# A state-space mixer's scan on one core: output tables moved behind the input tables, chunk inputs copied two groups at a time, a scan step of four full-width operations

## The chip, the cores and the metric

The kernel runs on one core of one Trainium2 chip. The metric is the device time of one execution in microseconds (us); the kernel before takes 2886.24 us (median of 3 runs, 2885.1 to 2886.93). Engines are named as in the profile: PE (TensorE matmul; PEld its weight loads), DVE (VectorE), ACT (ScalarE), POOL (GpSimd), SP (the queue that issues most DMAs). L353 means line 353 of the kernel.

## The reference, cut to what matters

The model is a two-layer encoder on 1040 tokens of width 1024. The change touches only the token mixer of layer 0, a bidirectional S5 state-space mixer. For each of 64 groups (16 channels, 64 complex states) and for each of two directions:

```
abar = exp(lambda * dt)                 # one complex number per group and state
bbar = (abar - 1) / lambda * b          # 64 x 16, complex
s[l] = abar * s[l-1] + bbar @ u[l]      # the scan over tokens l; the second direction runs backwards
y[l] = Re(c @ s[l])                     # summed over both directions
y    = y + d_skip * u, then GELU, a GLU and a projection
```

Everything behind it (GLU, projection, layer norms, SwiGLU, grouped-query attention, a second SwiGLU) is untouched.

## The kernel before, in words

The 1040 tokens are cut into NK = 130 chunks of T = 8. Within a chunk, the effect of inputs on outputs is a small matrix per group; across chunks a state per group is carried. All of that is `s5_phase` (L114 to L550), which runs alone at the start of the program; the rest of the kernel follows it. The order of instructions on each engine is the order in which the program issues them (written out by hand), and each engine works through its own list in order, waiting on semaphores for data and for buffers.

`s5_phase` has these stages.

1. **Parameters.** DVE computes `abar` and the coefficients into `AC`. PE transposes inputs (`x_main`, `x_tail`), the raw `b` and `c` parameters (`param_T`) and `AC`; ACT copies the results out of PSUM. DVE builds the powers of `abar` (`PW`, by `cmul`) and from them the input tables `G3` (`tables`, L299). POOL adds `Br` and `Bi` into `Hs` (L252). The two raw parameters share one buffer, so `raw_c` is loaded into it after `raw_b` has been transposed.
2. **Input side, 16 batches of four groups** (loop at L394). In batch `gb`: `x_main` transposes inputs (batches 2 to 9 only; `xg_copy` stages them on ACT in batches 1 to 8); `g_batch(gb + 1)` multiplies out the next batch's input matrices (five DVE operations of 128x512, L335 to L339, eight PE transposes, two ACT copies into `W`); `x_batch(gb)` multiplies `W` with the inputs `U` on PE (L353, L355: forward and backward halves, one PSUM bank a group), and ACT copies each group's result into `XS[:, k, c, g]`, the chunk inputs (L357, 128x258 each, four a batch). `XS` has the group as its last index, so each of these copies writes single 4-byte values 256 bytes or more apart.
3. **Output tables** (`out_side`, L367, on POOL): the sum `Cs`, a complex product into `PC` (`cmul`, six operations of 128x512) and four operations of `tables` into `E3`, with two ACT copies. It is issued in batches 1 and 6 of stage 2. From `E3` and `c`, `e_batch` (five POOL operations of 128x512, L386 to L390) makes the output matrices of four groups. Four of the 16 `e_batch` calls (EARLY) are issued in batch 10 of stage 2, the other twelve inside the scan.
4. **Scan** (L489): 128 dependent steps over the chunks, `i` = 2 to 129, on DVE. The state has 128 partitions (64 states of each direction) and, per partition, 2 x 64 values (real and imaginary part of 64 groups). A step is cut into two halves of 32 groups, six operations:

```
for h, gs in enumerate(halves):
    V.tensor_tensor(out=TA[:, h], in0=SB[:, :, :, gs], in1=bc(st[:, :, gs], 1, 2), op=ALU.mult)
for h, gs in enumerate(halves):
    V.tensor_tensor(out=bi[:, :, gs], in0=TA[:, h, 0], in1=bi[:, :, gs], op=ALU.add)
for h, gs in enumerate(halves):
    V.tensor_tensor(out=nx[:, :, gs], in0=bi[:, :, gs], in1=TA[:, h, 1, ::-1], op=ALU.add)
```

   `SB` (the real part twice, and plus and minus the imaginary part of `abar` to the eighth) and `bi` (the chunk inputs, copied four chunks at a time by ACT into `IN`, L484, two buffers) lie in PSUM; `TA`, `st` and `nx` lie in SBUF. So every operation of a step reads one operand from PSUM and one from SBUF.
   Beside the scan, POOL makes the output matrices (`e_batch`, paced by E_PACE steps), and for each batch `inside` computes the within-chunk part: POOL `dI` (L424), PE (L433), ACT copies (L439 to L441), POOL adds (L442, L443), eight DMAs `M0` on SP (L449), PE (L455), an ACT copy into `U` (L460). Its parts come 2, 6, 8, 18 and 21 steps after its start, which is at step 3 + 6.2 `gb`. In the second half of the scan `swap` turns the backward direction's states round, through a PSUM bank, on ACT.
5. **Output** (L528): PE multiplies the states with the output matrices (L534, 256 matmuls), DVE adds them to `U`, and the result goes to DRAM and back for GELU.

PSUM has eight banks: five for general use (`s5_ps`), three for `SB` and the two `IN` buffers.

Of the kernel before, what the change touches and what calls it, by code (L numbers as in the profile page):

```python
# [9 lines left out]
FP32 = mybir.dt.float32  # L10
# [3 lines left out]
ALU = mybir.AluOpType  # L14
# [4 lines left out]
KT = 8  # L19
G = 64  # L20
LATE_FT = 4
EARLY = 4
Y_AT = 18
X_AT, E_AT = 2, 10
E_PACE, L_PACE = 7.9, 6.2
CH = 16
T = 8
NK = L // T
# [2 lines left out]
def bc(ap, dim, n):  # L31

    a = ap.unsqueeze(dim)
    shape = list(a.shape)
    shape[dim] = n
    return a.to_broadcast(shape)
# [77 lines left out]
def s5_phase(nc, tc, P, a, ident, acc, xres, ydram, late):  # L114

    V, A, PE, PO = nc.vector, nc.scalar, nc.tensor, nc.gpsimd
    ps = P("s5_ps", bufs=5, space=PSUM)

    psc = P("s5_psc", space=PSUM)

    def bank(name="b"):
        return ps.tile([128, 512], FP32, tag="b", name=name)
# [70 lines left out]
    def x_tail():  # L193
        b = bank()
        transpose(b[:, :128], XT.rearrange("p t c -> p (t c)"))
        A.copy(out=U[:, :, 128:130], in_=b[:, :128].rearrange("p (k g) -> p g k", k=2))

    def param_T(x, raw):

        PT = tab.tile([128, 2, G, CH], FP32, name=x + "T")  # L200
        for h in range(4):
            b = bank()
            for c4 in range(4):
                c = 4 * h + c4
                transpose(b[:, c4 * 128:c4 * 128 + 128], raw[:, c::CH] if x == "b" else raw[:, c * 128:c * 128 + 128])
            A.copy(out=PT[:, :, :, 4 * h:4 * h + 4], in_=b.rearrange("p (c i g) -> p i g c", c=4, g=G))
        return PT[:, 0], PT[:, 1]
# [38 lines left out]
                lst[i]()  # L246
    for p in range(4):
        x_main(p, XG0[:, 4 * p:4 * p + 4])
    Br, Bi = param_T("b", raw_b)
    x_tail()  # L250
    Hs = tab2.tile([128, G, CH], FP32, name="Hs")
    PO.tensor_tensor(out=Hs, in0=Br, in1=Bi, op=ALU.add)  # L252
    AC = pc.tile([64, 4, 128], FP32, name="AC")
    cm, nr, sh, sn, t1, t2, rden = (t[n] for n in ("cm", "nr", "sh", "sn", "t1", "t2", "rden"))
    V.scalar_tensor_tensor(out=cm, in0=sh, scalar=-2.0, in1=sh, op0=ALU.mult, op1=ALU.mult)
# [25 lines left out]
    PO.memset(PW[:, 1, 0], 0.0)  # L281
    V.tensor_copy(out=PW[:, :, 1], in_=b[:, :128].rearrange("p (k g) -> p k g", k=2))
    A.copy(out=acT, in_=b[:, :256].rearrange("p (k g) -> p k g", k=4))
    P.close("s5_pc")
    XG1 = xg_copy(4, 4)
    for p in range(4):
# [28 lines left out]
    A.copy(out=dsk, in_=b[:CH, :G])  # L315
    Cs = tab.tile([128, G, CH], FP32, name="Cs")

    SB = psc.tile([128, 512], FP32, name="SB")[:, :256].rearrange("p (j c g) -> p j c g", j=2, g=G)
    A.copy(out=SB[:, 0], in_=bc(PW[:, 0, 8], 1, 2))
    A.copy(out=SB[:, 1, 0], in_=PW[:, 1, 8])  # L320
    A.mul(SB[:, 1, 1], PW[:, 1, 8], -1.0)


    xs_p = P("s5_xs", side="right")
    XS = xs_p.tile([128, NK, 2, G], FP32, name="XS")
# [20 lines left out]
        return W  # L346

    def x_batch(gb, W):
        for j in range(NB):
            b = bank()  # L350
            g = NB * gb + j
            for c2 in range(2):
                PE.matmul(b[0:64, c2 * NK:c2 * NK + NK - 1], W[:, j, c2, 0:64], U[:, g, 0:NK - 1],  # L353
                          start=True, stop=True)
                PE.matmul(b[64:128, c2 * NK:c2 * NK + NK - 1], W[:, j, c2, 64:128], U[:, g, NK - 1:0:-1],  # L355
                          start=True, stop=True)
            A.copy(  # L357
                out=XS[:, 1:NK, :, g].rearrange("p k c -> p c k"),
                in_=b[:, :2 * NK].rearrange("p (c k) -> p c k", c=2)[:, :, :NK - 1],
            )  # L360


    PC = pw_p.tile([128, 2, T, G], FP32, name="PC")
# [1 line left out]
    s2 = w2.rearrange("p (n g) -> p n g", g=G)  # L365

    def out_side():  # L367
        PO.tensor_tensor(out=Cs, in0=Cr, in1=Ci, op=ALU.add)
        cmul(nc, PC[:, 0], PC[:, 1], PW[:, 0, 0:8], PW[:, 1, 0:8], bc(acT[:, 2], 1, T), bc(acT[:, 3], 1, T), s1, s2, eng=PO)
        yield from tables(PO, E3, PC, slice(0, 8), slice(7, None, -1), -1)  # L370

    NG = G // NB
    ek = tab.tile([128, NB, T, CH], FP32, name="ek")
# [16 lines left out]
        PO.tensor_tensor(out=ei, in0=ei, in1=ek, op=ALU.subtract)  # L390

    W = g_batch(0)
    side = out_side()
    for gb in range(NG):  # L394
        p = 8 + gb - X_AT
        if 8 <= p < NG:
            x_main(p, nxg)
        if gb in (1, 6):
            next(side, None)
        if gb == E_AT:  # L400
            P.close("s5_xg", "s5_in", "s5_xin")
            Eh[0] = P("s5_e0", side="right").tile([128, 2, G // 2, T, CH], FP32, name="E0")
            for b in range(EARLY):
                e_batch(b)
        Wn = g_batch(gb + 1) if gb + 1 < NG else None
        if 7 <= p < NG - 1:
            nxg = xg_copy(p + 1, 1)
        x_batch(gb, W)
        W = Wn
    for q in range(4):  # L410
        dst = xres[q * 256:q * 256 + 256].rearrange("(g c) t k -> t c g k", c=CH)
        for t in range(T):
            nc.sync.dma_start(out=dst[t], in_=U[16 * t:16 * t + 16, 16 * q:16 * q + 16, :])
    P.close("s5_pw", "s5_g", "s5_tab2")


    Eh[1] = P("s5_e1", side="right").tile([128, 2, G // 2, T, CH], FP32, name="E1")
    rp = P("s5_r")
    TA = rp.tile([128, 2, 2, 2, G // 2], FP32, name="TA")
    def inside(gb):  # L420

        gs = slice(NB * gb, NB * gb + NB)
# [39 lines left out]
    def swap(lo, hi):  # L462

        n = hi - lo
        t = bank().rearrange("p (k c g) -> p k c g", c=2, g=G)[64:, :n]
        m0, m1 = NK - hi, NK - lo
        A.copy(out=t, in_=XS[64:, lo:hi])
        yield
        for cs, cp in [(slice(0, 2), A.copy)] if lo else [(slice(0, 1), A.copy), (slice(1, 2), V.tensor_copy)]:
            cp(out=XS[64:, lo:hi, cs], in_=XS[64:, m1 - 1:m0 - 1 if m0 else None:-1, cs])  # L470
            cp(out=XS[64:, m0:m1, cs], in_=t[:, ::-1, cs])
# [2 lines left out]
    cuts = [65, 61, 57, 53, 49, 45, 41, 37, 33, 29, 25, 21, 17, 13, 10, 7, 4, 0]  # L474
    sw = [(lo, hi) for hi, lo in zip(cuts, cuts[1:])]
    begun = []
    halves = [slice(0, G // 2), slice(G // 2, G)]
    IN = {}

    def inputs(i):  # L480
# [7 lines left out]
    inputs(2)  # L488
    for i in range(2, NK):  # L489
        for gb in range(NG):  # L490
            if i == 2 + int(E_PACE * (gb - EARLY)):
                e_batch(gb)
            l0 = 3 + int(L_PACE * gb)
            if i == l0:
                work[gb] = [inside(gb), l0]
        for gb in list(work):
            if i >= work[gb][1]:
                at = next(work[gb][0], None)
                if at is None:
                    del work[gb]  # L500
                else:
                    work[gb][1] = 3 + int(L_PACE * gb) + at
        if i % 4 == 2 and i + 4 < NK:
            inputs(i + 4)
        st, nx, bi = XS[:, i - 1], XS[:, i], IN.pop(i)
        for h, gs in enumerate(halves):
            V.tensor_tensor(out=TA[:, h], in0=SB[:, :, :, gs], in1=bc(st[:, :, gs], 1, 2), op=ALU.mult)  # L507
        for h, gs in enumerate(halves):
            V.tensor_tensor(out=bi[:, :, gs], in0=TA[:, h, 0], in1=bi[:, :, gs], op=ALU.add)  # L509
        for h, gs in enumerate(halves):  # L510
            V.tensor_tensor(out=nx[:, :, gs], in0=bi[:, :, gs], in1=TA[:, h, 1, ::-1], op=ALU.add)  # L511
        if sw and len(begun) < 2 and i > NK // 2:
            begun.append((sw[0][0], swap(*sw.pop(0))))
            next(begun[-1][1])
        while begun and NK - 1 - begun[0][0] <= i - 1:
            next(begun.pop(0)[1], None)
    for gb in list(work):
        for _ in work.pop(gb)[0]:
# [9 lines left out]
    for ft in range(KT):  # L528
# [11 lines left out]
        if ft % 2:  # L540
# [4 lines left out]
            if ft < LATE_FT:  # L545
                for f in (ft - 1, ft):
                    ys[f] = load_y(nc.scalar, y_p, ydram, f)
                for f in (ft - 1, ft):
                    gelu(nc, acc, ys[f], f)
    P.close("s5_e1", "s5_e0", "s5_xs", "s5_psc", "s5_ps", "s5_y")  # L550


def load_y(eng, pool, src, ft, tag="y"):
# [1036 lines left out]
```

## Time and profile before

| | |
|---|---|
| median of 3 runs | 2886.24 us |
| the profiled execution, its own time | 2882.8 us |
| its span, first to last instruction | 2881.0 us |
| busy share of the span | PE 92%, PEld 89%, DVE 55%, ACT 41%, POOL 19% |
| chain that ended last, by engine | PE 77%, DVE 14%, ACT 4%, issue 3%, DMA 1%, POOL 1% |
| DVE scan lines in that chain | L509 2%, L507 2%, L511 2% |
| output matmuls L534 in that chain | 2% |

The share of busy time is a mean over stages with different limits: PE is the bound of the long part behind `s5_phase`, and the mean says little about the first 330 us. The chain of work that ended last is followed back from the last instruction, at each step to what released it. The view by stretches, the timelines of single engines, the groups by line and the waits, from which the rows below are taken, give start times in us from the span's start.

### The profile page before, as it was taken

Reading aid. Unit: us, or ns where it says so; the run is one execution under the profiler, and the core shown is the slowest. Engines: PE = TensorE matmul, PEld = TensorE weight load, DVE = VectorE, ACT = ScalarE, POOL = GpSimd, SP = SyncE. Lnnn points to the kernel's source line nnn. Section 1 sums busy time; section 2 is a strip of 40 time slices with the busy share of each in tenths; the row PEclk is TensorE's granted clock in tenths of the full one; section 3 lists DMA queues with packets and bytes.
Section 4 is the critical chain, followed back from the end, with each engine's and each line's share of the span. In section 5 each row is a group of like instructions: output and inputs, shape, how many; then the busy total and the mean of one; then the engine's idle time right before and its main releaser. Section 6 shows DMA issues by size and latency. Waiting matters only on the chain.

```text
span 2881.0 us, 43478 instructions
## 1 busy us (share of the span) xinstructions
PE 2660.3 (92%) x17277; PEld 2560.6 (89%) x17277; DVE 1586.5 (55%) x3270; ACT 1168.4 (41%) x2170; POOL 545.2 (19%) x544
## 2 busy tenths in 40 slices
PE   6654999999999999998999998999999999999997
PEld 5544899999999999998988888888999999999996
DVE  8897353743333333338768888886473333333334
ACT  6545442532212221244558777775432121222225
POOL 3771142400000000024014443431230000000002
PEclk8776999999999999999999999999999999999998
DMA  5111664121111111101201011112111111111101
GB/s 131 28 36 31 192 208 148 52 81 45 45 45 52 52 52 52 45 30 65 99 12 41 21 38 49 23 23 90 34 47 45 51 44 52 45 45 45 44 30 59
DMA packets 124839, 167.44 MB, mean 58 GB/s; under 512 B 13499, under 2 KB 104971, under 8 KB 124635
## 3 DMA queue, kind: packets, MB, share of 16 engines
q1 hardware_dynamic: 118203, 141.22, 17.2%
q0 software_dynamic: 5712, 21.30, 2.2%
q8 instruction: 136, 2.23, 0.3%
q10 hardware_dynamic: 720, 2.13, 0.2%
q14 instruction: 68, 0.56, 0.1%
HBM read 126.41 MB, written 21.23 MB: 51 GB/s over the span
## 4 chain that ended last, share of the span: by engine, by line
PE 77%; DVE 14%; ACT 4%; issue 3%; DMA 1%; POOL 1%; SPq 0%; ACTq 0%; POOLq 0%; DVEq 0%
PE bk L696 21%; PE bk L695 21%; PE bk L697 21%; PE pv L1107 4%; PE pt L1085 3%; DVE mx L1065 2%; DVE pl L1098 2%; PE b L534 2%; DVE IN L509 2%; DVE TA L507 2%; DVE XS L511 2%; ACT ph L1093 1%; DVE acc L751 1%; ACT P L1069 1%; PE bk L917 1%
## 5 line engine op out<-in xcount | busy, mean ns | idle before, releaser
L695 PE MATMUL bk<-Hh,unit 128*128 128x348 f32 (+1 forms) x2928 | 956.1, 327 | 7.4 <-ACT Hh L785 3.8
L696 PE MATMUL bk<-Hl,unit 128*128 128x348 f32 (+1 forms) x2928 | 945.3, 323 | 1.3 <-DVE Hl L789 1.0
L697 PE MATMUL bk<-Hh,unit 128*128 128x348 f32 (+1 forms) x2928 | 943.7, 322 | 0.0
L695 PEld LDWEIGHTS bk<-Hh,unit 128*128 128x128 f32 x2928 | 555.1, 190 | 12.6 <-ACT vf L1477 3.8
L696 PEld LDWEIGHTS bk<-Hl,unit 128*128 128x128 f32 x2928 | 554.8, 189 | 6.8 <-DVE Hl L789 2.4
L697 PEld LDWEIGHTS bk<-Hh,unit 128*128 128x128 f32 x2928 | 554.7, 189 | 0.0
L859 DVE TENSOR_TENSOR sg<-sg,bk 128x348 f32<-128x348 f32 x132 | 68.0, 515 | 631.7 <-PE bk L697 623.9
L724 POOL TENSOR_TENSOR lns<-lns,lnsq 128x348 f32<-128x348 f32 (+1 forms) x72 | 70.0, 982 | 1550.9 <-ACT lnsq L722 1549.8
L695 PE MATMUL bk<-gt,unit 128*128 128x348 f32 (+1 forms) x1056 | 340.3, 322 | 0.0
L697 PE MATMUL bk<-gt,unit 128*128 128x348 f32 (+1 forms) x1056 | 338.9, 321 | 0.0
L696 PE MATMUL bk<-gt,unit 128*128 128x348 f32 (+1 forms) x1056 | 338.3, 320 | 0.0
L882 DVE TENSOR_TENSOR acc<-acc,bk 128x348 f32<-128x348 f32 (+1 forms) x480 | 237.3, 512 | 112.5 <-PE bk L697 112.5
L861 ACT CAST gt<-sg 128x348 fp32r<-128x348 f32 x132 | 63.6, 482 | 490.0 <-DVE sg L859 490.0
L1085 PE MATMUL pt<-ident,P 128*116 128x128 f32 (+1 forms) x1188 | 181.6, 279 | 44.0 <-DVE pl L1098 38.7
L1098 DVE TENSOR_TENSOR pl<-pt,ph 116x512 fp32r<-116x512 f32 (+3 forms) x340 | 204.2, 618 | 15.1 <-ACT ph L1093 13.1
L1073 POOL TENSOR_SCALAR P<-P,l 128x1044 f32<-128x1044 f32 x132 | 149.9, 1148 | 293.3 <-PE pv L1107 170.0
L1085 PEld LDWEIGHTS pt<-ident,P 128*116 128x116 f32 (+1 forms) x1188 | 132.7, 136 | 80.5 <-issue 32.4
L696 PEld LDWEIGHTS bk<-gt,unit 128*128 128x128 f32 x1056 | 198.7, 188 | 0.5 <-issue 0.2
L695 PEld LDWEIGHTS bk<-gt,unit 128*128 128x128 f32 x1056 | 198.7, 188 | 0.5 <-issue 0.2
L610 ACT CAST unit<-raw 128x1024 fp32r<-128x1024 f32 x110 | 113.1, 1046 | 211.1 <-DMA raw<-in_ffn_w_up_dram 166.2
L1093 ACT CAST ph<-pt 116x512 fp32r<-116x512 f32 (+3 forms) x340 | 168.7, 535 | 73.9 <-PE pt L1085 59.8
L697 PEld LDWEIGHTS bk<-gt,unit 128*128 128x128 f32 x1056 | 198.6, 188 | 0.0
(286 smaller groups left out, 4053.7 us busy)
## 6 DMA issues: line engine op xcount, KB each, us to landing
raw<-in_ffn_w_gate_dram SPq DMA_DIRECT2D x44, 512.0 KB
raw<-in_ffn_w_up_dram SPq DMA_DIRECT2D x44, 512.0 KB
raw<-in_ffn_w_down_dram SPq DMA_DIRECT2D x44, 512.0 KB
y<-xdram SPq DMA_DIRECT2D x16, 520.0 KB
QA<-QH SPq DMA_DIRECT2D x30, 260.0 KB
raw<-in_attn_w_qkv_dram SPq DMA_DIRECT2D x14, 512.0 KB
xdram<-acc SPq DMA_DIRECT2D x32, 130.0 KB
xres<-xn POOLq DMA_DIRECT2D x8, 520.0 KB, 5.1
```

What stands on the lines that cost most here:

```text
L610: A.copy(out=u[:, 0], in_=r)
L695: mm(out, wh, xh, start=(first and i == 0), stop=False)
L696: mm(out, wh, xl, start=False, stop=False)
L697: mm(out, wl, xh, start=False, stop=(last and i == n - 1))
L724: (nc.vector if on_dve else nc.gpsimd).tensor_tensor(out=part, in0=part, in1=sq, op=ALU.add)
L859: V.tensor_tensor(out=sg, in0=sg, in1=bu, op=ALU.mult)
L882: V.tensor_tensor(out=x, in0=x, in1=b, op=ALU.add)
L1073: PO.tensor_scalar(out=k.P, in0=k.P, scalar1=k.l, scalar2=1.0, op0=ALU.mult, op1=ALU.mult)
L1085: PE.transpose(b[:m, w * i + 128 * x:w * i + 128 * x + 128], u.P[x][:, KB_N * kt:KB_N * kt + m], self.ident)
L1093: A.copy(out=u.ph[s][:m, :w], in_=u.t[s][:m, :w])
L1098: V.tensor_tensor(out=u.pl[s][:m, :w], in0=u.t[s][:m, :w], in1=u.ph[s][:m, :w].bitcast(FP32), op=ALU.subtract)
L1107: PE.matmul(u.o[:, :u.w], VAs[u.j][:m, kt], (u.ph, u.pl)[x][s][:m, c:c + u.w], start=(kt == 0 and x == 0), stop=(kt == KBS - 1 and x == 1))
```

## The change

- Parameters: the transposes of `b`, `x_tail` and the sum `Hs` are issued behind the transposes of `AC` and the copies of its result, instead of ahead of them.
- Output tables: `out_side` runs on DVE instead of POOL, in one piece, and is issued only in the last batch of the input side, behind the last `g_batch`. No `e_batch` is issued before the scan; all 16 are issued inside it, one every 6.0 steps from step 2 on (12 were, one every 7.9). `inside` starts at step 10 + 6.2 `gb` (L_AT) instead of 3 + 6.2 `gb`.
- Chunk inputs: `x_batch` writes two groups into a tile of two PSUM banks, and one ACT copy (128x516) brings both to `XS`, two neighbouring groups at a time. PSUM: four general banks (five before) and two such tiles (four banks) during the input side; these are closed before the scan, and only then are the bank of `SB` and `TB`, the two `IN` buffers and a bank of their own for `swap` opened. The three ACT copies that fill `SB` move there.
- Scan step: four operations of 128x128 instead of two of 128x128 and four of 128x64. One new product, `TB`, is written to PSUM, into the tile of `SB`; the sum `TS` goes to SBUF instead of back into `IN`. `swap` has one exchange under way instead of two.

```diff
-EARLY = 4
-E_PACE, L_PACE = 7.9, 6.2
+E_PACE, L_PACE, L_AT = 6.0, 6.2, 10
...
-    ps = P("s5_ps", bufs=5, space=PSUM)
-
-    psc = P("s5_psc", space=PSUM)
+    ps = P("s5_ps", bufs=4, space=PSUM)
+    psx = P("s5_psx", bufs=2, space=PSUM)
...
-    Br, Bi = param_T("b", raw_b)
-    x_tail()
-    Hs = tab2.tile([128, G, CH], FP32, name="Hs")
-    PO.tensor_tensor(out=Hs, in0=Br, in1=Bi, op=ALU.add)
     AC = pc.tile([64, 4, 128], FP32, name="AC")
...
     A.copy(out=acT, in_=b[:, :256].rearrange("p (k g) -> p k g", k=4))
+    Br, Bi = param_T("b", raw_b)
+    x_tail()
+    Hs = tab2.tile([128, G, CH], FP32, name="Hs")
+    PO.tensor_tensor(out=Hs, in0=Br, in1=Bi, op=ALU.add)
...
     def x_batch(gb, W):
-        for j in range(NB):
-            b = bank()
-            g = NB * gb + j
-            for c2 in range(2):
-                PE.matmul(b[0:64, c2 * NK:c2 * NK + NK - 1], W[:, j, c2, 0:64], U[:, g, 0:NK - 1],
-                          start=True, stop=True)
-                PE.matmul(b[64:128, c2 * NK:c2 * NK + NK - 1], W[:, j, c2, 64:128], U[:, g, NK - 1:0:-1],
-                          start=True, stop=True)
-            A.copy(
-                out=XS[:, 1:NK, :, g].rearrange("p k c -> p c k"),
-                in_=b[:, :2 * NK].rearrange("p (c k) -> p c k", c=2)[:, :, :NK - 1],
-            )
+        for j0 in range(0, NB, 2):
+            b = psx.tile([128, 2, 512], FP32, tag="bx", name="bx")
+            g = NB * gb + j0
+            for j in range(2):
+                for c2 in range(2):
+                    PE.matmul(b[0:64, j, c2 * NK:c2 * NK + NK - 1], W[:, j0 + j, c2, 0:64], U[:, g + j, 0:NK - 1],
+                              start=True, stop=True)
+                    PE.matmul(b[64:128, j, c2 * NK:c2 * NK + NK - 1], W[:, j0 + j, c2, 64:128], U[:, g + j, NK - 1:0:-1],
+                              start=True, stop=True)
+            A.copy(out=XS[:, 1:NK, :, g:g + 2],
+                   in_=b[:, :, :2 * NK].rearrange("p g (c k) -> p k c g", c=2)[:, :NK - 1])
...
     def out_side():
-        PO.tensor_tensor(out=Cs, in0=Cr, in1=Ci, op=ALU.add)
-        cmul(nc, PC[:, 0], PC[:, 1], PW[:, 0, 0:8], PW[:, 1, 0:8], bc(acT[:, 2], 1, T), bc(acT[:, 3], 1, T), s1, s2, eng=PO)
-        yield from tables(PO, E3, PC, slice(0, 8), slice(7, None, -1), -1)
+        cmul(nc, PC[:, 0], PC[:, 1], PW[:, 0, 0:8], PW[:, 1, 0:8], bc(acT[:, 2], 1, T), bc(acT[:, 3], 1, T), s1, s2)
+        for _ in tables(V, E3, PC, slice(0, 8), slice(7, None, -1), -1):
+            pass
+        V.tensor_tensor(out=Cs, in0=Cr, in1=Ci, op=ALU.add)
...
-        if gb in (1, 6):
-            next(side, None)
...
-            for b in range(EARLY):
-                e_batch(b)
-        Wn = g_batch(gb + 1) if gb + 1 < NG else None
+        if gb + 1 < NG:
+            Wn = g_batch(gb + 1)
+        else:
+            Wn = None
+            out_side()
...
+    P.close("s5_psx")
+    psc = P("s5_psc", space=PSUM)
+    psw = P("s5_psw", space=PSUM)
+
+    SBT = psc.tile([128, 4, 2, G], FP32, name="SB")
+    SB, TB = SBT[:, :2], SBT[:, 2]
+    A.copy(out=SB[:, 0], in_=bc(PW[:, 0, 8], 1, 2))
+    A.copy(out=SB[:, 1, 0], in_=PW[:, 1, 8])
+    A.mul(SB[:, 1, 1], PW[:, 1, 8], -1.0)
...
-    TA = rp.tile([128, 2, 2, 2, G // 2], FP32, name="TA")
+    TA = rp.tile([128, 2, G], FP32, name="TA")
+    TS = rp.tile([128, 2, G], FP32, name="TS")
...
-        t = bank().rearrange("p (k c g) -> p k c g", c=2, g=G)[64:, :n]
+        t = psw.tile([128, 4, 2, G], FP32, tag="t", name="t")[64:, :n]
...
-            if i == 2 + int(E_PACE * (gb - EARLY)):
+            if i == 2 + int(E_PACE * gb):
                 e_batch(gb)
-            l0 = 3 + int(L_PACE * gb)
+            l0 = L_AT + int(L_PACE * gb)
...
-        for h, gs in enumerate(halves):
-            V.tensor_tensor(out=TA[:, h], in0=SB[:, :, :, gs], in1=bc(st[:, :, gs], 1, 2), op=ALU.mult)
-        for h, gs in enumerate(halves):
-            V.tensor_tensor(out=bi[:, :, gs], in0=TA[:, h, 0], in1=bi[:, :, gs], op=ALU.add)
-        for h, gs in enumerate(halves):
-            V.tensor_tensor(out=nx[:, :, gs], in0=bi[:, :, gs], in1=TA[:, h, 1, ::-1], op=ALU.add)
-        if sw and len(begun) < 2 and i > NK // 2:
+        V.tensor_tensor(out=TA, in0=SB[:, 0], in1=st, op=ALU.mult)
+        V.tensor_tensor(out=TB, in0=SB[:, 1], in1=st, op=ALU.mult)
+        V.tensor_tensor(out=TS, in0=TA, in1=bi, op=ALU.add)
+        V.tensor_tensor(out=nx, in0=TS, in1=TB[:, ::-1], op=ALU.add)
+        if sw and not begun and i > NK // 2:
```

## Rows read from the trace of the kernel before

**Rows 1.** Stretches of the span: each engine's busy us, granted PE clock, DMA share, GB/s.

```profile
57.00:80.00 23.00, 20.89 (x263) 17.64 (x261) 22.42 (x37) 22.67 (x47) 3.48 (x1) 1.00 0.25 48
80.00:117.20 37.20, 27.45 (x280) 23.50 (x282) 30.27 (x21) 22.86 (x45) 34.90 (x24) 0.77 0.16 30
117.20:270.80 153.60, 70.61 (x640) 56.87 (x636) 143.44 (x769) 77.71 (x165) 76.96 (x103) 0.68 0.16 35
```

**Rows 2.** Timeline of DVE in stage 2: start, duration, line, idle before and releaser.

```profile
59.90 0.68 DVE L339 TENSOR_TENSOR k<-k,k 128x512 f32<-128x512 f32 x1
60.50 0.67 DVE L335 TENSOR_TENSOR k<-Hs,G 128x512 f32<-128x512 f32 x1
...
85.56 1.76 DVE L339 TENSOR_TENSOR k<-k,k 128x512 f32<-128x512 f32 x1
```

**Rows 3.** Timeline of POOL: the first early batch's second operation; two batches' starts in the scan.

```profile
80.77 1.11 POOL L387 TENSOR_TENSOR E<-cT,E 128x512 f32<-128x512 f32 x1 [6.58 <-PE b L126]
...
163.12 1.09 POOL L386 TENSOR_TENSOR ek<-Cs,E 128x512 f32<-128x512 f32 x1
...
170.00 1.09 POOL L386 TENSOR_TENSOR ek<-Cs,E 128x512 f32<-128x512 f32 x1
```

**Rows 4.** Timeline of PE: arrival of c, first x_batch's last matmul, two pairs of batches.

```profile
30.97 3.65 PE L126 MATMUL b<-ident,raw_c 128*128 128x128 f32 x16 [4.08 <-DMA raw_c<-in_s_c_im_dram]
...
39.24 0.27 PE L353 MATMUL b<-acc,W 128*64 128x129 f32 x1
...
60.18 0.66 PE L126 MATMUL b<-ident,XG 128*128 128x128 f32 x4
...
63.55 0.66 PE L126 MATMUL b<-ident,XG 128*128 128x128 f32 x4
...
83.44 1.10 PE L126 MATMUL b<-ident,k 128*128 128x128 f32 x8
...
86.38 0.66 PE L126 MATMUL b<-ident,k 128*128 128x128 f32 x4
```

**Rows 5.** ACT copies: timeline of one batch, then groups by line.

```profile
61.72 1.07 ACT L345 COPY W<-b 128x512 f32<-128x512 f32 x2
...
63.19 2.03 ACT L357 COPY XS<-b 128x258 f32<-128x258 f32 x4
...
L357 ACT COPY XS<-b 128x258 f32<-128x258 f32 x21 | 10.8, 684 | 0.0
...
L191 ACT COPY acc<-b 128x512 f32<-128x512 f32 x8 | 4.6, 588 | 3.4 <-PE b L126 3.4
...
L196 ACT COPY acc<-b 128x128 f32<-128x128 f32 x1 | 0.3, 280 | 2.1 <-PE b L126 2.1
```

**Rows 6.** ACT, a contiguous copy of nearly the size of L357's, inside the scan.

```profile
L460 ACT COPY acc<-b 128x260 f32<-128x260 f32 x32 | 10.3, 372 | 0.1
```

**Rows 7.** Timeline of DVE: the first scan steps.

```profile
118.47 0.49 DVE L509 TENSOR_TENSOR IN<-TA,IN 128x64 f32<-128x64 f32 x2 [0.33 <-ACT IN L484]
...
119.27 0.48 DVE L507 TENSOR_TENSOR TA<-SB,XS 128x128 f32<-128x128 f32 x2
119.66 0.48 DVE L509 TENSOR_TENSOR IN<-TA,IN 128x64 f32<-128x64 f32 x2
120.18 0.35 DVE L511 TENSOR_TENSOR XS<-IN,TA 128x64 f32<-128x64 f32 x2
120.45 0.48 DVE L507 TENSOR_TENSOR TA<-SB,XS 128x128 f32<-128x128 f32 x2
```

**Rows 8.** Timeline of DVE in stage 1: operations of 128x128, and the wait ahead of them.

```profile
21.03 0.29 DVE L282 COPY PW<-b 128x128 f32<-128x128 f32 x1 [5.59 <-PE b L126]
...
22.87 0.28 DVE L107 TENSOR_TENSOR w<-PW 128x128 f32<-128x128 f32 x1
23.19 0.29 DVE L108 TENSOR_TENSOR PW<-w,w 128x128 f32<-128x128 f32 x1
```

**Rows 9.** Waits in the scan: who waited for whom, us in total, times, longest.

```profile
PE b L455 <- DMA M<-Z: 21.6, 3, 9.7
```

More of the change, by code (lines that the diff above doesn't have):

```diff
@@ L316, in s5_phase @@
     Cs = tab.tile([128, G, CH], FP32, name="Cs")
[L318 to L321, printed above, removed]
     xs_p = P("s5_xs", side="right")
@@ L392, in s5_phase @@
     W = g_batch(0)
-    side = out_side()
     for gb in range(NG):
@@ L476, in s5_phase @@
     begun = []
-    halves = [slice(0, G // 2), slice(G // 2, G)]
     IN = {}
@@ L501, in s5_phase @@
                 else:
-                    work[gb][1] = 3 + int(L_PACE * gb) + at
+                    work[gb][1] = L_AT + int(L_PACE * gb) + at
         if i % 4 == 2 and i + 4 < NK:
@@ L505, in s5_phase @@
         st, nx, bi = XS[:, i - 1], XS[:, i], IN.pop(i)
-        for h, gs in enumerate(halves):
-            V.tensor_tensor(out=TA[:, h], in0=SB[:, :, :, gs], in1=bc(st[:, :, gs], 1, 2), op=ALU.mult)
-        for h, gs in enumerate(halves):
-            V.tensor_tensor(out=bi[:, :, gs], in0=TA[:, h, 0], in1=bi[:, :, gs], op=ALU.add)
-        for h, gs in enumerate(halves):
-            V.tensor_tensor(out=nx[:, :, gs], in0=bi[:, :, gs], in1=TA[:, h, 1, ::-1], op=ALU.add)
-        if sw and len(begun) < 2 and i > NK // 2:
+        V.tensor_tensor(out=TA, in0=SB[:, 0], in1=st, op=ALU.mult)
[3 more added lines that the diff above has]
+        if sw and not begun and i > NK // 2:
             begun.append((sw[0][0], swap(*sw.pop(0))))
             next(begun[-1][1])
-        while begun and NK - 1 - begun[0][0] <= i - 1:
+        if begun and NK - 1 - begun[0][0] <= i - 1:
             next(begun.pop(0)[1], None)
@@ L549, in s5_phase @@
                     gelu(nc, acc, ys[f], f)
-    P.close("s5_e1", "s5_e0", "s5_xs", "s5_psc", "s5_ps", "s5_y")
+    P.close("s5_e1", "s5_e0", "s5_xs", "s5_psw", "s5_psc", "s5_ps", "s5_y")
 def load_y(eng, pool, src, ft, tag="y"):
```

## The prediction

> **What bounds the kernel now.** I read the view by stretches first, because the change touches only the first 330 us and the page's shares are means over the whole span. In the stretch of the input side from 57 to 80, PE (20.9 of 23 us), DVE (22.4) and ACT (22.7) are all nearly full and POOL is almost idle. From 80 to the scan, POOL is full (34.9 of 37.2), PE's granted clock falls to 0.77 and ACT has idle time: something else sets the pace. In the scan DVE is busy 143 of 154 us [rows 1]. The DVE timeline says what changed at 80: an operation of `g_batch` starts 0.60 after the one before it as long as POOL is idle, and lasts 1.76 once POOL works on `e_batch` [rows 2, 3]. Both engines then take turns. Five operations a batch are 3.0 us undisturbed and about 8.4 (five times 1.76 less the same 0.08 of overlap) beside POOL. So today the input side is bound by DVE wherever POOL runs, and by PE and ACT elsewhere. The scan is bound by the start-to-start times of its own six DVE operations: a step takes 120.45 - 119.27 = 1.18 us [rows 7].
>
> **The start, ahead of the input side.** Issuing `AC`'s transposes ahead of `b`'s takes DVE's 5.59 us wait ahead of L282 away [rows 8], nearly all of it, since that wait was for transposes behind a late input. I count it at nothing: PE's next chain begins when `c` has landed, at 30.97, with DVE already behind its first tables, and ends with the last matmul of the first `x_batch` at 39.24 [rows 4]. `c` goes into `b`'s buffer, and `b` is now transposed about 1 us later; if the load waits for that, up to 1 us is lost. `Hs` on POOL now meets DVE's table arithmetic and may block it for the length of an operation or two, which the removed wait covers.
>
> **The input side, with POOL silent.** No POOL operation runs beside `g_batch` any more, so DVE takes 5 x 0.60 = 3.0 us a batch. PE: two batches with input transposes start 63.55 - 60.18 = 3.37 us apart at full clock, and without them 86.38 - 83.44 = 2.94 [rows 4]. ACT today makes four copies of 128x258 at (2.03 - 0.68) / 3 = 0.45 each, plus four of 128x512 (two `W`, one `XG`, one `acc`) at about 0.5 [rows 5].
>
> The price of the new 128x516 copy is in no row. From below: a 128x512 copy with contiguous output lasts 0.59. From above: two of the old, 2 x 0.68 = 1.37 [rows 5]. The old one is slow for its size: 258 elements take 0.68, or 0.37 (260) where the output is contiguous [rows 6], so scattered 4-byte writes cost something. The new copy writes pairs, 8 bytes. The copy of `x_tail` (L196) writes pairs as well, and its 128 elements last 0.28 [rows 5], which is in line with 0.37 for 260: no penalty visible. I take 0.60, 0.55 start to start. ACT then needs 4 x 0.5 + 2 x 0.55 = 3.1 us a batch, under PE's 3.37. So PE sets the pace of batches 2 to 9 and PE or DVE (2.94, 3.0; DVE may run two batches ahead) that of the rest.
>
> Sum from PE's timeline: end of the first `x_batch` 39.4; batch 1, 2.9; batches 2 to 9, 8 x 3.37 = 27.0; batches 10 to 14, 5 x 2.94 = 14.7; batch 15, products only, 2.94 - 1.03 = 1.9. That gives 85.9. Behind it stand the last copy (0.7 with its wait), the three copies into `SB`, now behind it (0.28 for the 128-element one, 0.8 at most together), and the copy into `IN` (0.6): the first add of the scan starts at 88.0. Now it starts at 118.47 [rows 7]. **Gain 30.5 us.**
>
> `out_side` on DVE is ten operations at 0.60 and `Cs` at twice that, 7.2 us. I count it at nothing: DVE has finished `g_batch(15)` when PE is about to transpose it, near 78, so it ends near 85 to 86, under PE's last two batches and the copies. Without that cover it costs at most its 7.2 us. Its two ACT copies (0.6 each) stand in the queue ahead of the last `XS` copies and wait for the product only. Fewer general PSUM banks (four for three uses a batch) leave one spare; I count nothing.
>
> **The scan.** POOL now has 16 batches instead of 12, 170.00 - 163.12 = 6.88 us each with the adds for `inside` [rows 3], or 110 us; a batch is issued every 6.0 steps, about 6.9 us, so POOL is nearly full but keeps up. All `inside` starts move 7 steps, with eight DMAs each on SP's queue; behind a late one PE's L455 waits, behind that ACT's L460, and behind that the copies into `IN`, for which DVE would wait. Today PE waited 21.6 us for those DMAs [rows 9] and DVE not at all. The spacing of steps within a batch is unchanged, and the last copy into `U` comes at step 124 of 129, still ahead of the end. Nothing is added there.
>
> The step itself: two operations of 128x128 that don't depend on each other start 0.48 - 0.28 = 0.20 apart (the `TA` pair). One that needs the result just ahead of it starts 23.19 - 22.87 = 0.32 later [rows 7, 8]. In the new step `TS` to `nx` and `nx` to the next `TA` are such pairs. Between `TA` and `TB`, and between `TB` and `TS`, no data passes. But today the two `IN` adds, on separate halves of one PSUM tile, start 0.48 - 0.22 = 0.26 apart, while the equally long `XS` pair, which goes to SBUF, starts 0.35 - 0.22 = 0.13 apart; and `XS` starts 0.26 behind the second `IN` though it needs only the first [rows 7]. So an access to a PSUM tile that is being written, or was just read, waits for its neighbour in the tile. `TB` is written into the tile of `SB`, which `TA` reads: either that pair waits (0.32), or the wait comes behind the PSUM write, between `TB` and `TS`. I take one of the two: 0.20 + 3 x 0.32 = 1.16 us a step against 1.18, **gain 128 x 0.02, about 3 us**. Bounds: neither waits, 1.04 (18 us gained); both wait, 1.28 (13 us lost).
>
> The Trainium skill (VectorE: DVE Perf Modes, The DRAIN you can't avoid) says that the next operation doesn't start until the pipe of the one before is empty. The `TA` pair at 0.20 with 0.28 of duration speaks against that for independent operations, the pairs at 0.32 agree. By that rule the new step would be the 1.28 of the upper bound, which is rival A below.
>
> **The rest.** Output stage and all that follows keep their order and start earlier by the sum. Total 30.5 + 3 = 33.5. The profiled execution took 2882.8, so 2849.3; the median of the runs lies 3.4 above it: **2852.7 us**.
>
> **Rivals.**
> A: all four operations of the step wait, 1.28. For it: the 0.26 spacings. Against: one rule explains those with a single wait. 128 x 0.12 more than forecast, 15 us: 2868.
> B: the 516-element copy is slow, because it reads two banks alternately or pays for each pair. At 0.9 start to start ACT needs 3.8 and sets batches 2 to 9: 8 x 0.43 = 3.5; at 1.37 without overlap 4.7 and, without input copies, 3.7: 8 x 1.3 + 5 x 0.8 = 14. So 2856 to 2867. L196 speaks against.
> C: neither PSUM pair waits, 1.04: 2837. The 0.26 of `IN` speaks against.
> D: POOL's fuller queue falls behind. If its operations take 1.6 instead of 1.2, as beside `g_batch`, 16 batches take 144 us, and the last `inside` runs some 15 to 20 us past the scan: 2870. Against: beside the scan they keep 6.88.
> E, the slower side: the step's operations block on POOL as `g_batch`'s do. Each blocked operation costs 1.76 - 0.68, about 1.1 us. One a step, with POOL busy three quarters of the scan, is 128 x 0.8 = 102 us: 2955. It decides from 33.5 / 128 = 0.26 us a step. Against: each new operation reads one input from PSUM, as each of today's does, and today's steps run beside a busy POOL without a trace of it. The Trainium skill (SBUF, SBUF: two separate sides) says that the lock on the port shared with GpSimd needs two SBUF inputs on VectorE; the trace agrees.
>
> **Chances.** Forecast 0.64 (its own range 2847 to 2858: 1 us at the start, the copies, cover of `out_side`); A 0.13, B 0.10, C 0.06, D 0.04, E 0.03. The range 2840 to 2868 takes in the forecast, A and B and leaves out C, D and E, 0.13, and the forecast's tails. Slower by over 0.2% (5.8 us, about what a measurement of this kernel can tell from no change) only E and mishaps unlisted: 0.04; within it 0.01; faster 0.95.
>
> **What would show it.** In the new profile: `g_batch` operations at 0.60 throughout and PE's clock at full from 40 to 86; L357's copy near 0.6; the first `TS` near 88; ten `out_side` operations behind the last L339 and no DVE idle time behind them longer than about 2 us; steps of 1.16 with `TB` or `TS` starting 0.32 behind its neighbour; no DVE wait for `IN`; L534 starting about 33 us earlier. The prediction is wrong if ACT has no idle time in batches 2 to 9, if DVE waits for ACT or POOL inside the scan, or if a step takes over 1.4 us.

## The result, and the profile after

The changed kernel takes 2844.91 us (median of 4 runs, 2844.66 to 2845.95) against 2886.59 of the kernel before beside it (2885.1 to 2887.89): a ratio of 0.9859, interval 0.9844 to 0.9873. The forecast was 2852.7 with a range of 2840 to 2868, and 2847 to 2858 for the likeliest case alone; the time lies in the first and 2 us below the second. In two more sets of runs the same kernel took 2848.1 (before there 2885.39) and 2847.83 (2888.02), so the gain was 41.7, 37.3 and 40.2 us, where 33.5 had been forecast.

The profiled execution took 2844.93 us, span 2843.2. The view by stretches, with the columns of [rows 1]: PE busy, PEld, DVE, ACT, POOL, granted PE clock, DMA share, GB/s.

```profile
31.00:57.00 26.00, 26.00 (x324) 23.18 (x323) 26.00 (x44) 23.60 (x45) 0.00 (x0) 0.97 0.56 112
57.00:80.00 23.00, 23.00 (x313) 20.46 (x313) 22.36 (x37) 19.23 (x35) 0.00 (x0) 1.00 0.31 58
...
100.00:150.00 50.00, 29.34 (x264) 21.95 (x266) 45.58 (x173) 16.63 (x40) 46.86 (x58) 0.74 0.18 37
150.00:230.00 80.00, 39.84 (x312) 29.46 (x306) 72.98 (x275) 55.09 (x114) 42.50 (x57) 0.67 0.19 44
```

From 57 to 80, PE is now busy without a gap (23.00 of 23, 20.89 in [rows 1]) and ACT has come down from 22.67 to 19.23 us: the input side is bound by PE, though DVE (22.36) has little to spare. POOL is silent up to the scan and nearly full in its first part. The clock from 57 to 80 is 1.00, the upper of its two levels, and 0.97 ahead of it.

The timeline of DVE, the stretch that answers to [rows 2] and [rows 7]: start, duration, operation, idle time before it.

```profile
74.70 0.68 DVE L332 TENSOR_TENSOR k<-k,k 128x512 f32<-128x512 f32 x1
75.31 0.68 DVE L105 TENSOR_TENSOR w<-PW,acT 128x512 f32<-128x512 f32 x1
...
82.03 1.23 DVE L363 TENSOR_TENSOR Cs<-cT 128x1024 f32<-128x1024 f32 x1
84.59 0.29 DVE L507 TENSOR_TENSOR TA<-SB,XS 128x128 f32<-128x128 f32 x1 [1.33 <-ACT SB L414]
84.92 0.30 DVE L508 TENSOR_TENSOR SB<-SB,XS 128x128 f32<-128x128 f32 x1
85.13 0.28 DVE L509 TENSOR_TENSOR TS<-TA,IN 128x128 f32<-128x128 f32 x1
85.44 0.29 DVE L510 TENSOR_TENSOR XS<-TS,SB 128x128 f32<-128x128 f32 x1
85.76 0.29 DVE L507 TENSOR_TENSOR TA<-SB,XS 128x128 f32<-128x128 f32 x1
```

The last `g_batch` operation ends at 75.38, `out_side` follows at once and ends at 83.26, and DVE then waits 1.33 us for `SB`: the move of the tables to DVE is covered. L508 is the product `TB`, shown under the name of the tile that it lies in. Within a step `TB` starts 0.33 behind `TA`, `TS` 0.21 behind `TB`, `nx` 0.31 behind `TS` and the next `TA` 0.32 behind `nx`: 1.17 in all. One of the two PSUM pairs waits, as assumed, and it is `TA` to `TB`. The first add of the scan starts at 85.13, where 88.0 was forecast and 118.47 measured before [rows 7].

ACT's timeline of one batch, the answer to [rows 5]:

```profile
41.26 0.63 ACT L181 COPY XG<-XK 128x512 f32<-128x512 f32 x1
41.78 0.63 ACT L351 COPY XS<-bx 128x516 f32<-128x516 f32 x1
42.61 0.62 ACT L351 COPY XS<-bx 128x516 f32<-128x516 f32 x1 [0.20 <-PE bx L349]
...
44.63 0.63 ACT L181 COPY XG<-XK 128x512 f32<-128x512 f32 x1
```

The copy whose price stood in no row takes 0.62 to 0.63, no more than the contiguous 128x512 copies beside it; 0.60 had been taken. Even at this dense point of the input side ACT waits for PE, and the batches are 44.63 - 41.26 = 3.37 apart, PE's spacing.

The start and the output stage, from the timelines of DVE and PE; the first row answers to [rows 8], the second to the first of [rows 4]. The last fence is the output stage of the kernel before.

```profile
15.86 0.29 DVE L276 COPY PW<-b 128x128 f32<-128x128 f32 x1 [0.37 <-PE b L124]
```

```profile
28.42 3.65 PE L124 MATMUL b<-ident,raw_c 128*128 128x128 f32 x16 [5.67 <-DMA raw_c<-in_s_c_im_dram]
...
234.83 57.20 PE L533 MATMUL b<-XS,E 128*128 128x130 f32 x256 [17.15 <-ACT XS L473]
```

```profile
270.85 57.20 PE L534 MATMUL b<-XS,E 128*128 128x130 f32 x256 [22.36 <-ACT XS L471]
```

The output products start at 234.83; before it was 270.85. These 36.0 us are nearly all of the 37.9 between the two profiled executions (2882.8 and 2844.93). Of the waits between 85 and 240 (who waited for whom, us, times, longest), three rows:

```profile
ACT IN L485 <- DVE TS L509: 50.0, 17, 4.1
...
PE b L457 <- DMA M<-Z: 25.7, 7, 5.0
...
DVE acc L535 <- PE b L533: 3.1, 2, 1.8
```

PE still waits for the DMAs of `inside` (25.7 us, 21.6 in [rows 9]), ACT waits for DVE's buffers, and no row has DVE waiting for `IN`: the scan is bound by DVE's own start times, as before.

### The profile page after: what moved, and what is told of

It reads as the page before. It is cut to its first block, busy times and chain, and to the rows that moved or that the text cites. A ratio compares the mean times of both kernels' runs of the same rounds, so it can differ in the third digit from the quotient of the medians.

```text
span 2843.2 us, 43155 instructions
## 1 busy us (share of the span) xinstructions
PE 2649.4 (93%) x17277; PEld 2546.5 (90%) x17277; DVE 1559.1 (55%) x3025; ACT 1154.3 (41%) x2138; POOL 515.3 (18%) x533
## 4 chain that ended last, share of the span: by engine, by line
PE 78%; DVE 13%; ACT 4%; issue 3%; DMA 2%; POOL 1%; SPq 0%; ACTq 0%; DVEq 0%; POOLq 0%
PE bk L694 22%; PE bk L695 22%; PE bk L696 22%; PE pv L1106 4%; PE pt L1084 3%; DVE mx L1064 3%; DVE pl L1097 2%; PE b L533 2%; ACT ph L1092 1%; DVE TA L507 1%; DVE SB L508 1%; DVE XS L510 1%; PE bx L347 1%; PE b L124 1%; DVE TS L509 1%
```

## The experiments

My theory behind the prediction: the tables' absence from POOL gives the input side its gain, up to PE's pace, which the wider copies then make reachable; the step gains little because one PSUM pair waits; the start gives nothing. The rivals were that the gain is the copies', that the wait in the step lies behind the PSUM write itself, and that an operation of the step could block on POOL. Four runs do one part of the change alone.

**The output tables alone** (p_tables): `out_side` on DVE behind the last `g_batch`, no early `e_batch`, the paces of the changed kernel; everything else as before.

```diff
-EARLY = 4
-E_PACE, L_PACE = 7.9, 6.2
+EARLY = 0
+E_PACE, L_PACE, L_AT = 6.0, 6.2, 10
...
-        Wn = g_batch(gb + 1) if gb + 1 < NG else None
+        if gb + 1 < NG:
+            Wn = g_batch(gb + 1)
+        else:
+            Wn = None
+            out_side()
```

> The kernel before with the output tables' part alone: tables on DVE behind the last input batch, all 16 output-matrix batches inside the scan at the new paces. My theory (POOL beside DVE's two-SBUF-input products is what cost the time): DVE's products start 0.60 apart throughout; ACT with the old copies then sets batches 2 to 9 at about 3.8 us, PE or DVE the others at 3.0; the scan starts 26 to 29 us earlier than in the kernel before and the time falls by as much. Rival (the copies were the limit): under 15 us, because ACT holds all batches near 3.8 or more.

Measured: 2855.43 against 2885.23, ratio 0.99 (0.9887 to 0.9913), 29.8 us gained. The stretch from 57 to 80, columns as above, the landing of `c` and DVE's first adds of the scan:

```profile
57.00:80.00 23.00, 22.21 (x292) 19.17 (x292) 20.95 (x36) 23.00 (x51) 0.00 (x0) 1.00 0.45 89
```

```profile
29.66 3.65 PE L126 MATMUL b<-ident,raw_c 128*128 128x128 f32 x16 [4.29 <-DMA raw_c<-in_s_c_im_dram]
```

```profile
90.33 0.49 DVE L511 TENSOR_TENSOR IN<-TA,IN 128x64 f32<-128x64 f32 x2 [0.33 <-ACT IN L486]
```

With POOL silent and the old copies ACT is full, 23.00 of 23, where the changed kernel has PE full. In this run `c` landed at 29.66, so the first add comes 60.67 us behind it; in the kernel before it is 118.47 - 30.97 = 87.50, in the changed kernel 85.13 - 28.42 = 56.71. Counted from `c`, the silent POOL is worth 26.8 us on the input side, and the copies 4.0 on top.

**The copies alone** (p_copies): two groups a copy, the two-bank tiles and the one exchange of `swap`, with POOL's tables left where they were.

```diff
-        for j in range(NB):
-            b = bank()
+        for j0 in range(0, NB, 2):
+            b = psx.tile([128, 2, 512], FP32, tag="bx", name="bx")
...
```

> The kernel before with the chunk inputs' part alone: two groups a copy of 516 elements, SB and its banks filled behind them, one exchange under way. My theory: only the five or so batches in which POOL is silent get shorter, from 3.8 to 3.4 us, some 2 us, less the 0.7 us of the SB copies, so 1 to 3 us faster; from the first output-matrix batch on DVE beside POOL sets the pace as before. Rival (the copies were the limit): 10 us faster or more.

Measured: 2885.79 against 2885.23, ratio 0.9997 (0.9985 to 1.0009): no difference that can be measured in the medians. One of its 12 runs took 2868.22, 12.6 us below the next; it has no profile and stays unexplained. The profiled run shows more than copies that bring nothing. POOL's first table operation, `Cs`, was kept out by DVE for 27.60 us (see the last section), so POOL's tables came late, and ACT's copies of them, which stand in ACT's list ahead of the copies for the next batches, held up ACT, then PE, then DVE:

```profile
64.53 1.25 ACT L306 COPY E<-PC 64x512 f32<-64x512 f32 x2 [9.38 <-POOL PC L108]
...
67.57 1.11 PE L125 MATMUL b<-ident,XG 128*128 128x128 f32 x4 [10.26 <-ACT XG L182]
...
69.57 0.73 DVE L330 TENSOR_TENSOR k<-bT,G 128x512 f32<-128x512 f32 x1 [11.05 <-PE b L125]
```

So 0 alone and 4 behind the other part is what was measured, but the 0 is no price of the copies by themselves: this run mixes them with a stall. That a lighter ACT is worth nothing because POOL's work holds DVE back, as had been expected, isn't shown by it.

**The step alone** (p_step): four operations, `TB` in the tile of `SB`.

```diff
+    SBT = psc.tile([128, 4, 2, G], FP32, name="SB")
+    SB, TB = SBT[:, :2], SBT[:, 2]
...
+        V.tensor_tensor(out=TA, in0=SB[:, 0], in1=st, op=ALU.mult)
+        V.tensor_tensor(out=TB, in0=SB[:, 1], in1=st, op=ALU.mult)
+        V.tensor_tensor(out=TS, in0=TA, in1=bi, op=ALU.add)
+        V.tensor_tensor(out=nx, in0=TS, in1=TB[:, ::-1], op=ALU.add)
...
```

> The kernel before with the scan step of four full-width operations alone, TB in the tile of SB. My theory: a step of 1.17 us for 1.185, 2 to 3 us faster. Rival (every operation waits for the one ahead): 1.28 a step, 12 us slower. Rival (no wait between the PSUM operations): 1.04, 18 us faster.

Measured: 2882.59 against 2885.23, ratio 0.9994 (0.9986 to 1.0003). The forecast of 3 us lies in the interval, zero does too. The size is better read from the spacing, 1.167 a step for 1.185.

**The start alone** (p_start): `AC`'s transposes and copies ahead of `b`'s transposes, `x_tail` and `Hs`, the first part of the change's diff.

```diff
-    Br, Bi = param_T("b", raw_b)
...
     AC = pc.tile([64, 4, 128], FP32, name="AC")
...
+    Br, Bi = param_T("b", raw_b)
```

> The kernel before with the reordered start alone: transposes of b and the tail, and Hs, behind the transposes of AC. My theory: DVE's wait ahead of its first copy of the powers goes (about 5 us), but the transposes of c start when c has landed, at 28 to 31 us, and the time is the same within 1 us; the earlier landing of c in the changed kernel's profile is how long the loads took in that execution. Rival (the reordering lets c land earlier): c lands at about 28.4 and the time falls by 2.5 us.

Measured: 2881.64 against 2885.23, ratio 0.999 (0.9981 to 0.9998). That is 0.6 to 5.5 us faster, where nothing had been counted. So the reorder was taken out of the changed kernel, and the changed kernel ran again beside it:

```diff
+    Br, Bi = param_T("b", raw_b)
+    x_tail()
+    Hs = tab2.tile([128, G, CH], FP32, name="Hs")
+    PO.tensor_tensor(out=Hs, in0=Br, in1=Bi, op=ALU.add)
     AC = pc.tile([64, 4, 128], FP32, name="AC")
...
```

> The changed kernel with only the reorder at the start undone: b's transposes, x_tail and Hs stand ahead of AC's transposes again. If the reorder is worth what the reordered kernel of before showed (2.9 us, interval 0.6 to 5.5), this is 3 us slower than the changed kernel run beside it, and DVE waits some 5 us ahead of L282's copy again. If the reorder is worth nothing, as the prediction counted, both take the same time within 1.5 us, and the time at which c lands varies from run to run in both orders alike. If the later transposes of b cost the load of c (up to 1 us in the prediction), this is up to 1 us faster.

> The changed kernel again, unedited, as the neighbour of the kernel without the reorder: 2845 to 2848, as in its two earlier sets of runs. Both theories give the same here; the difference to the neighbour decides.

Measured: 2848.35 (2846.96 to 2851.44) without the reorder and 2847.83 (2846.65 to 2848.99) with it, 0.5 us apart, with four runs of each that overlap; a difference of 2 us would hardly show. DVE waits ahead of its copy again, as the first of these rows (u_start) shows; the others are `c`'s arrival without the reorder and, in the second fence, with it.

```profile
20.29 0.29 DVE L280 COPY PW<-b 128x128 f32<-128x128 f32 x1 [4.84 <-PE b L124]
...
29.98 3.59 PE L124 MATMUL b<-ident,raw_c 128*128 128x128 f32 x16 [3.81 <-DMA raw_c<-in_s_c_im_dram]
```

```profile
31.92 3.27 PE L124 MATMUL b<-ident,raw_c 128*128 128x128 f32 x16 [3.14 <-DMA raw_c<-in_s_c_im_dram]
```

The 4.84 us return and cost nothing that shows: what comes next waits for `c`. And `c` lands at a time that changes from run to run. In the profiles with the old order it landed at 30.97, 29.66, 28.77, 29.82 and 29.98, in those with the new order at 29.51, 28.42, 29.43, 31.92, 29.14, 26.79 and 28.20. The unedited changed kernel alone has 28.42, 29.43 and 31.92. In its profiles the scan's first product follows 56.17, 55.89 and 55.94 us behind it: a late `c` moves the whole input side. Most of p_start's 2.9 us may be this scatter (its first add came 2.04 earlier than before's, its `c` 1.46); the rest of it stays open, and the last section has another part that such medians can hold.

**Where the step waits** (after_again, d1_tb_bank, d2_tb_sbuf, d3_halves; one set of runs, before there 2885.39). The first is the changed kernel unedited, as the neighbour. The second gives `TB` a PSUM tile, and with it a bank, of its own; `swap` goes back to the general banks. The third puts `TB` into SBUF, which takes the same wait away and makes both inputs of the last sum SBUF. The fourth goes back to six operations in two halves, but gives each half's `IN` a tile of its own; for the banks, `swap`'s exchange moves to SBUF and three general banks are left of four.

```diff
 # second
-    SB, TB = SBT[:, :2], SBT[:, 2]
+    SB = SBT[:, :2]
+    TB = psw.tile([128, 4, 2, G], FP32, name="TB")[:, 0]
 # third
-    SB, TB = SBT[:, :2], SBT[:, 2]
+    SB = SBT[:, :2]
+    TB = rp.tile([128, 2, G], FP32, name="TB")
 # fourth
-        t = psc.tile([128, 4, 2, G], FP32, tag="in", name="IN", bufs=2)
-        A.copy(out=t[:, :n], in_=XS[:, i:i + n])
+        for h, gs in enumerate(halves):
+            t = psc.tile([128, 4, 2, G // 2], FP32, tag=f"in{h}", name=f"IN{h}", bufs=2)
+            A.copy(out=t[:, :n], in_=XS[:, i:i + n, :, gs])
...
```

> The changed kernel once more, on the chip of the next three. Both theories on the start of the input side are asked again: if the landing of c is how long the loads took in one execution, it lies anywhere from 28.4 to 31.0 us here; if the reordered start sets it, at 28.4 again. Time 2845 to 2848 us.

> The changed kernel with TB in a PSUM bank of its own (swap's exchange goes back to the general banks). My theory (an operation waits for its neighbour because both touch one PSUM tile): TB starts 0.20 behind TA, a step is 1.04 us, 128 x 0.12 = 16 us less for DVE; POOL's 6.88 us a batch against 6.2 us for six steps makes the last batches late, so 11 to 16 us of it show in the time. Rival (a PSUM write itself takes 0.12 longer than one to SBUF): the step stays at 1.17.

> The changed kernel with TB in SBUF, so that the last sum of a step reads two SBUF operands. My theory (DVE and POOL take turns when both their operations read SBUF only): TB starts 0.20 behind TA, but the last sum waits for POOL whenever POOL has work, up to 1.1 us each; over the 110 us of POOL work that is one wait a POOL operation, 80 to 110 waits of 0.3 to 1.1 us, 40 to 100 us slower than the changed kernel. Rival (no taking of turns at these sizes): 1.04 a step, 11 to 16 us faster.

> The changed kernel with the six operations in two halves of the kernel before, but each half's chunk inputs in a PSUM tile of its own (swap's exchange through SBUF). My theory: with no neighbour in the same tile every operation follows at its own length, 0.20 + 0.20 + 4 x 0.13 = 0.92 us a step for 1.17; DVE's part of the scan falls to 118 us, which is less than POOL's 110 plus the 20 steps behind its last batch, so 15 to 25 us show in the time and DVE begins to wait for ACT's copies. Rival (halves are slow by themselves): 1.06 or more a step.

Measured: 2848.1 (ratio 0.987, 0.9854 to 0.9886); 2833.01 (0.982, 0.9805 to 0.9834); 2873.02 (0.996, 0.9945 to 0.9974); 2831.28 (0.9813, 0.9798 to 0.9827). DVE's timeline in d1_tb_bank:

```profile
87.34 0.29 DVE L508 TENSOR_TENSOR TA<-SB,XS 128x128 f32<-128x128 f32 x1
87.55 0.29 DVE L509 TENSOR_TENSOR TB<-SB,XS 128x128 f32<-128x128 f32 x1
87.75 0.28 DVE L510 TENSOR_TENSOR TS<-TA,IN 128x128 f32<-128x128 f32 x1
88.06 0.29 DVE L511 TENSOR_TENSOR XS<-TS,TB 128x128 f32<-128x128 f32 x1
88.38 0.29 DVE L508 TENSOR_TENSOR TA<-SB,XS 128x128 f32<-128x128 f32 x1
```

`TB` still goes to PSUM and now starts 0.21 behind `TA`; a step is 1.04. The wait belonged to the shared tile, not to the PSUM write. 128 x (1.167 - 1.04) is 16.3 us, and 15.1 were measured. The two programs show what it is. In the changed kernel DVE waits on its own count of finished operations ahead of `TB`; with a tile of its own that wait is not there:

```
L507 TENSOR_TENSOR TA<-SB,XS 128x128 [waits DVE_49]
L508 TENSOR_TENSOR SB<-SB,XS 128x128 [waits DVE_49]
L509 TENSOR_TENSOR TS<-TA,IN 128x128
L510 TENSOR_TENSOR XS<-TS,SB 128x128 [waits DVE_49]

L508 TENSOR_TENSOR TA<-SB,XS 128x128 [waits DVE_49]
L509 TENSOR_TENSOR TB<-SB,XS 128x128
L510 TENSOR_TENSOR TS<-TA,IN 128x128 [waits DVE_49]
L511 TENSOR_TENSOR XS<-TS,TB 128x128 [waits DVE_49]
```

So the program itself asks for an order between two uses of one PSUM tile, though they touch different parts of it, and that is enough to explain the time: behind this wait `TB` starts 0.33 behind `TA`, as `nx` and the next `TA` do (0.31, 0.32) behind results that they need. Whether the chip would hold the pair without the wait isn't shown, since in these runs a tile of its own was a bank of its own too. The same listing explains why `TS` waits for nothing in the changed kernel: `TA` had already been waited for by `TB`.

In d2_tb_sbuf, `TB` starts 0.21 behind `TA` as well, so its undisturbed step is that of d1_tb_bank. Yet it takes 40.0 us more. The groups of DVE between 84 and 235, then one step in the timeline of DVE and what POOL did at that time:

```profile
L511 DVE TENSOR_TENSOR XS<-TS,TB 128x128 f32<-128x128 f32 x106 | 69.8, 658 | 3.7
L508 DVE TENSOR_TENSOR TA<-SB,XS 128x128 f32<-128x128 f32 x106 | 30.9, 291 | 4.9 <-ACT SB L414 1.3
```

```profile
121.05 0.29 DVE L508 TENSOR_TENSOR TA<-SB,XS 128x128 f32<-128x128 f32 x1
121.26 0.28 DVE L509 TENSOR_TENSOR TB<-SB,XS 128x128 f32<-128x128 f32 x1
121.46 0.28 DVE L510 TENSOR_TENSOR TS<-TA,IN 128x128 f32<-128x128 f32 x1
121.77 2.36 DVE L511 TENSOR_TENSOR XS<-TS,TB 128x128 f32<-128x128 f32 x1
```

```profile
121.82 1.09 POOL L379 TENSOR_TENSOR ek<-Cs,E 128x512 f32<-128x512 f32 x1
122.88 1.09 POOL L380 TENSOR_TENSOR E<-cT,E 128x512 f32<-128x512 f32 x1
124.05 1.26 POOL L381 TENSOR_TENSOR E<-ek,E 128x512 f32<-128x512 f32 x1
```

Only the operation with two SBUF inputs is held: it takes 658 ns in the mean, against 287 in d1_tb_bank, while the other three keep theirs. The one that starts at 121.77 ends at 124.13, when POOL's second operation is over (123.97). 106 x 0.37 is 39 us, nearly the whole difference. This is rival E's mechanism, which the change avoids with `TB` in PSUM.

In d3_halves an undisturbed step is 0.92, some 15 us less than 1.04 over 128 steps, but the kernel is only 1.7 us faster than d1_tb_bank, which their intervals don't separate: with its waits the scan takes 1.03 a step in the mean, 1.04 in d1_tb_bank. Waits and stretches of d3_halves in the scan:

```profile
ACT f L440 <- POOL dI L443: 25.6, 13, 4.4
...
DVE IN L511 <- ACT IN L486: 10.1, 9, 2.0
```

```profile
84.00:134.00 50.00, 28.48 (x246) 19.87 (x248) 49.60 (x317) 19.52 (x56) 47.96 (x55) 0.67 0.12 26
134.00:184.00 50.00, 30.27 (x294) 23.26 (x288) 41.97 (x265) 33.95 (x79) 47.73 (x59) 0.79 0.19 40
```

POOL is full (47.96 and 47.73 of 50), ACT waits for it, and DVE waits for ACT's copies into `IN`, 10.1 us in 9 times. This is a chain of rival D's kind, which the changed kernel escapes. A step below POOL's pace doesn't bring it about at once: in d1_tb_bank six steps take 6.2 us and a batch of POOL 6.9, and DVE waits for `IN` once, for 0.2 us. At 5.5 us for six steps it shows.

## Why the prediction was right

The sign and the mechanism were right, and the time lay in the range.

- **Start, counted at 0.** Nothing speaks against it in the changed kernel, 0.5 us with and without it; p_start's 0.6 to 5.5 us on the kernel before isn't explained by it. `Hs` did block DVE, for one operation (2.33 us at 18.88, where its neighbours take 0.29), under the cover that was named.
- **Input side, 30.5.** It gained 118.47 - 85.13 = 33.3. Of this 2.55 is `c`, which landed at 28.42 instead of the 30.97 that the sum began with. From `c` on, 57.0 had been forecast and 56.7 came. Of the 87.50 - 56.71 = 30.8 us gained from `c` on, 26.8 come with the silent POOL alone (p_tables) and 4.0 with the copies.
- **Copies.** 0.63 for the taken 0.60; the bound of 1.37 was far off, and L196 was the row to go by. ACT waits for PE, so rival B falls.
- **`out_side`, 0.** Confirmed by DVE's 1.33 us wait for ACT behind it.
- **Step, 1.16 and 3 us.** 1.167, so about 2.3 us. That one pair waits was right; where was left open, and it is `TA` to `TB`. The prediction read the wait off spacings as what an access to a busy tile does; the listing above shows that the program asks for it. Rival A (1.28) falls. Rival C (1.04) is not what the change does, but is to be had by giving `TB` the bank of `swap` (d1_tb_bank).
- **POOL in the scan, 0.** No DVE wait for `IN`; rival D falls here.
- **Rival E.** It doesn't occur in the change. Where it was brought about it cost 40.0 / 128 = 0.31 us a step, above the 0.26 from which it decides, but less than the 0.8 worked out; why a held sum waits 0.37 in the mean and not the 1.1 of a `g_batch` operation wasn't settled.

The mis-sized term is the total's last one, the 3.4 us from the profiled execution to the median. In the profiles themselves the sum holds: the output products start 36.0 us earlier, and 36.0 less `c`'s 2.55 is 33.5, as forecast. But the profile of before lay 3.4 below its median, as the prediction noted, and the profile of after (2844.93) lies at its own (2844.91), so carrying the 3.4 over was wrong. Three executions of the changed kernel show how far one can stray: their spans are 2843.2, 2847.1 and 2846.4, with `c` between 28.42 and 31.92 and the part from the output products to the end at 2608.4, 2611.5 and 2608.3 (2610.2 before). Which of these made the medians' gains 37.3 to 41.7 rather than 33.5 can't be told with one profile of the kernel before, and stays open. The last section names one more candidate, some 5 us that executions with POOL's tables ahead of the scan can lose and the profile of before did not.

The Trainium skill (VectorE: DVE Perf Modes, The DRAIN you can't avoid) says that the next operation waits for the pipe to be empty, and adds that one which isn't held starts earlier. The prediction used the first half alone for the 1.28 of rival A. The runs bear out the addition too: pairs without a wait between them start 0.20 to 0.21 apart with 0.29 of duration in d1_tb_bank, those with one 0.31 to 0.33. The Trainium skill (SBUF, SBUF: two separate sides) says that a VectorE operation in a 2-port mode or with two SBUF inputs, the latter only against a GpSimd operation that reads SBUF, and a GpSimd operation lock each other out of the port pair that they share. d2_tb_sbuf agrees as to the two inputs, 658 ns against 287 for the same sum.

## What to carry to other kernels

Work taken off one engine can be worth most to another that takes turns with it: here 29.8 of some 40 us came from a POOL that is silent while DVE works on the input tables, and the lighter ACT copies paid 4 us on top of that. In a chain of short dependent operations look at start-to-start times, not durations, and give each intermediate that is live together with another its own PSUM tile (here also a bank): 0.12 us a step was 15 us here, and the version with `TB` in a tile of its own (2833.01) is better than both kernels. Before a sum is corrected from a profile to a median, see how far the landing of a load ahead of the chain moves from run to run.

## What the runs showed that was not expected

POOL can be kept out for long. In p_step, and likewise in p_copies (27.60 us), the sum `Cs` on POOL started while DVE's `g_batch` operations followed each other, and lasted far longer than the 3.73 us of the kernel before. POOL's timeline, then DVE's:

```profile
33.95 24.77 POOL L369 TENSOR_TENSOR Cs<-cT 128x1024 f32<-128x1024 f32 x1 [12.94 <-ACT cT L206]
```

```profile
55.20 0.68 DVE L340 TENSOR_TENSOR k<-k,k 128x512 f32<-128x512 f32 x1
55.81 0.68 DVE L336 TENSOR_TENSOR k<-Hs,G 128x512 f32<-128x512 f32 x1
56.61 2.66 DVE L337 TENSOR_TENSOR k<-bT,G 128x512 f32<-128x512 f32 x1
59.19 1.75 DVE L338 TENSOR_TENSOR k<-bT,G 128x512 f32<-128x512 f32 x1
```

DVE runs at 0.60 a start, undisturbed, until one operation starts 0.80 behind its predecessor; POOL gets in at that gap, and from then on both alternate at about 1.7 us each. In this run one short gap in DVE's stream stands between a POOL that is kept waiting and a DVE at less than half its pace. What opened the gap, and whether a gap is always what it takes, was not tried: in p_copies POOL got in where DVE waited 11.05 us for PE, in the kernel before behind a start at 0.63.

It matters for the medians. From the landing of `c` to the first add of the scan p_step took 122.20 - 29.82 = 92.4 us and p_copies 120.87 - 28.77 = 92.1, where POOL was kept out; the kernel before took 87.5 and p_start 116.43 - 29.51 = 86.9, where `Cs` lasted 3.73 and 2.62 us. p_step leaves the input side as it was, so these 5 us can come and go by themselves. How often the unprofiled runs of the kernel before lost them is not known; it may be part of why the gains came out above 33.5, and of p_start's 2.9.
